# Mixer B's recurrence: E's product over the whole array, and the outputs of four steps in one PSUM bank

## The chip, the core and the metric

The kernel runs on one core of a Trainium2 chip, in one launch. The metric is the device time of that launch in microseconds (us); several runs are taken and their median is compared. TensorE (PE) multiplies matrices and writes to PSUM, eight banks of 512 float32 values on each of 128 partitions. VectorE (DVE) and ScalarE (ACT) read and write PSUM and the on-chip memory SBUF, GpSimd (POOL) only SBUF; SyncE (SP) issues most of the transfers. Each engine works through its own queue in order, and semaphores tie the queues together.

## What is computed

One inference step of a two-layer backbone over 128 prompt tokens and 1024 latent tokens, model width 1024, all in float32. Layer 0 has windowed attention (mixer A) beside a bidirectional recurrence (mixer B), layer 1 differential attention (mixer C); each layer has a modulated norm ahead, a gate, an out projection and a residual. This case is about mixer B: 8 heads of 64 channels, forward and backward. The reference for one direction:

```python
def rwkv_scan(S0, r, decay, kk, a, k, v, reverse):
    def step(S, inp):
        r_t, w_t, kk_t, a_t, k_t, v_t = inp
        sa = jnp.einsum('bhvk,bhk->bhv', S, -kk_t)
        S = (S * w_t[:, :, None, :] + sa[..., None] * (kk_t * a_t)[:, :, None, :]
             + v_t[..., None] * k_t[:, :, None, :])
        return S, jnp.einsum('bhvk,bhk->bhv', S, r_t)
```

The outputs of both directions are added, normed, gated and go into layer 0's out projection.

## The kernel before

**Chunks and items.** The recurrence isn't run token by token but in chunks of 64. Within a chunk the dependence between tokens is a triangular system; its inverse R is formed ahead for all chunks, so that a *step* of the scan handles a chunk by a few matrix products. An `Item` is 512 tokens in either direction: items 0 to 7 are the two halves of the latent sequence for each of four pairs of heads (8 steps each, both directions in one step), item 8 is the prompt of all four pairs (four lanes of two chunks, 8 steps in all). The two heads of a pair lie on the two halves of the 128 partitions. So there are 72 steps; 68 of them have a state coming in, the first step of each prompt lane has none.

**Stages of an item.** `b_prep` makes decays, keys and queries. `b_front` (once a direction) transposes them on PE into `py` tiles (L988), forms the products between keys and queries of a chunk in a `pa` tile of two banks (L998), and masks them on DVE (L1004 to `za`, L1006 to `q`), two tiles of 128 tokens at a time. `b_subst` transposes `za` to `mp` on DVE (L1032) and solves 32 by 32 blocks on POOL, 62 small instructions in a row (L1039, L1041). `b_invert` turns these back on DVE (L1050), completes R by two rounds of small products (L1061, L1068), forms E from R in another `pa` tile (L1081, scaled by DVE at L1085), and R's product with the values, which becomes `VU` (L1095). `b_scan` is the recurrence. `b_finish` norms and gates two items' sum.

**A step of the scan** (`b_scan`, L1101 to L1145), for both directions d:

- E's product, L1115: E of the chunk (64 columns) against the state G, to half the partitions of a `sc` bank; DVE adds it to `VU` (L1116).
- The update of the state, L1119: `kb` against `VU`, 128 by 128; DVE adds the old state (L1126), ACT scales it by the decay to the next S (L1128). The next step's E's product needs G.
- The outputs, to a `py` tile: S against the queries `zr` (L1132, 128 columns), then `VU` against `q` for either head (L1134, 64 columns, one half of the partitions each). For each direction DVE adds the 64 columns to `y` (L1140) or, where nothing is there yet, ACT copies them (L1142).

**PSUM before:** `pa` 2 tiles of 2 banks, `py` 2 of one bank (transposes, low-rank products, modulation and the scan's outputs share them), `sc` 2 of one bank. All eight banks are taken. Beside item 7 `out_part` multiplies the first half of layer 0's out projection, in `pa` tiles of two halves (L770 to L783).

**What sets the order.** While item i is scanned, item i+1 is inverted, item i+2 goes through front and substitution and item i+3 through prep; a hand-written table of times (`TIMES`, `T7`, `T8`, in shares of an item) interleaves the generators' steps in `timeline`. From that program a scheduler with a model of the engines' times makes each engine's queue, so neighbours on a queue can stand in another order than in the code; two products into one bank keep their order. The scan's products thus lie between pieces of fronts, inversions and the modulation (L287, `adaw`), which fills PE throughout. `mp`, `rp` and `Rt` have one buffer each; L1050 is also put behind the last DVE instruction of the neighbouring items' earlier work by a manual order (`behind`).

Of the kernel before, what the change touches and what calls it, by code (L numbers as in the profile page):

```python
# [13 lines left out]
AF = mybir.ActivationFunctionType  # L14
# [5 lines left out]
P = 128  # L20
# [121 lines left out]
def hybrid_step(ctx: ExitStack, tc: tile.TileContext, I, O, stop=99):  # L142
    nc = tc.nc
    PE, VE, AE, GE, SP = nc.tensor, nc.vector, nc.scalar, nc.gpsimd, nc.sync
    def behind(ins, others):
        """issue ins after the others, earlier instructions of its engine"""
        for o in others:
            if o is not None:
                tc.add_manual_dep(ins.ins, o.ins.name, mybir.DependencyInfo(
                    mybir.DependencyClass.NoSync, mybir.DependencyReason.DATA), reason="order")  # L150
# [36 lines left out]
    def zipped(a, na, b, nb):  # L187
        """both generators to their ends, in step"""
# [74 lines left out]
    # ------------------------------------------------------------ modulation  # L263
# [48 lines left out]
    def mod_gate(l, psum, tag, rows):  # L312
        """the gates' rows to DRAM"""
# [6 lines left out]
    # ------------------------------------------------------------ pre-norm, transposed and split  # L320
# [3 lines left out]
    def normed(xs, pool):  # L324
        """three tiles of rows over their root mean squares, in place"""
# [8 lines left out]
    def modulated(i, xs, pool, psum, hh, hl):  # L334
        """the three tiles transposed, modulated and split, to third i of the tokens"""
# [12 lines left out]
    # ------------------------------------------------------------ projections, three passes  # L348
# [60 lines left out]
    # ------------------------------------------------------------ layer 0, part 1: projections and mixer A  # L409
# [22 lines left out]
    def low_rank(m, z, pool):  # L432
        """half z of the inputs of the low-rank products to lowT, split and one part above the other"""
# [11 lines left out]
    def lora_split(z, pool):  # L445
        """both parts of the weights of half z of the low-rank products to loraT, each twice"""
# [94 lines left out]
    def a_group(g, hh, hl, wp, rp, ap, psum, rope, idb, msk):  # L541
        """mixer A of four heads, in steps: a tile is projected, its queries and keys are turned a step later, its
        scores follow when the next tile's keys are there, and its values behind them"""
# [37 lines left out]
        def near(t):  # L581
            """runs of keys, values, and masks (column, kind) of the queries of tile t"""
# [140 lines left out]
    # ------------------------------------------------------------ out projections  # L723
    RA, RB = VE, VE

    class Out:
        """weights and gates of the out projection of layer l, in pools to be closed"""
# [6 lines left out]
        def load_first(s, pool):  # L734
            """the first four steps of the contraction, to tiles that mixer C's weights take over"""
# [7 lines left out]
        def load(s, n):  # L743
            """the next n steps of the contraction"""
# [12 lines left out]
    def out_lhs(t, yT, ks, pool):  # L757
        """rows ks of tile t of the transposed input, split"""
# [8 lines left out]
    def out_part(out, pool, psum):  # L767
        """the product over the first half of the rows, to out.part"""
        for t in PART:
            yh, yl = out_lhs(t, yT0, range(4), pool)  # L770
            yield
            ps = tl(psum, [P, 2, 512], "pa")
            for j in range(2):
                w = slice(512 * j, 512 * j + 512)
                for k in range(4):
                    wh, wl = out.w[k]
                    PE.matmul(ps[:, j], yh[:, k], wh[:, w], start=k == 0, stop=False)
                    PE.matmul(ps[:, j], yh[:, k], wl[:, w], start=False, stop=False)
                    PE.matmul(ps[:, j], yl[:, k], wh[:, w], start=False, stop=k == 3)
# [6 lines left out]
    def out_tile(out, t, yT, res, pool, banks):  # L786
        """rows of token tile t behind a layer, in steps"""
# [40 lines left out]
    def out_rows(out, pool, psum):  # L828
        """the rows behind layer 0, to x1d and out.done"""
# [7 lines left out]
    # ------------------------------------------------------------ layer 0, part 2: mixer B  # L837
# [12 lines left out]
    class Item:  # L850
        """512 tokens of mixer B in either direction: half the latent sequence of one pair of heads (chunks of 64 in
        line), or the prompt of all four pairs (lanes of two chunks)."""
# [6 lines left out]
        def lanes(s, d):  # L859
            """(pair, columns, tokens)"""  # L860
# [4 lines left out]
        def chunks(s, x, d, scan=False):  # L865
            """[P, 512] in the order of the tokens (or of the scan) as [P, tiles, 2, 64] in the order of the scan"""
# [16 lines left out]
    def lanes_of(it, x, dram, blk, tok):  # L883
        """the item's columns x and its rows in DRAM, of blocks from blk on"""
# [3 lines left out]
    def b_prep(it, d, pool, pre, ps_y, rmask):  # L888
        """decays, and keys and queries under them, in direction d"""
# [72 lines left out]
    def b_front(it, d, pool, pre, ps_y, ps_a, vmask):  # L962
        """the products between the keys and queries of a chunk, and what the recurrence needs in its layout"""
# [80 lines left out]
    def b_invert(it, Rt, pool, pre, ps_s, ps_a):  # L1044
        """the rest of R with two products; then R against what enters before the state"""
# [29 lines left out]
        VE.tensor_scalar(De[:, :, 1:8:w], it.D[:, :, 0:7:w], -0.5, None, op0=ALU.mult)  # L1075
        it.E = tl(pool, [P, 2, 8, 64], "E", bufs=2)
# [7 lines left out]
        for e in range(2):  # L1084
            VE.tensor_tensor(it.E[:, :, 1 - e:8:2].rearrange("p d x t -> p (d x) t"),  # L1085
# [15 lines left out]
    def b_scan(it, lanes, H0, ring, ps_s, ps_y):  # L1101
# [5 lines left out]
        for i in range(it.steps):  # L1107
            for l in lanes:
                x, a = (l, i) if it.nl > 1 else (i // 2, i % 2)
                c, e = 2 * x + a, half_of(1 - a)  # L1110
                ps = tl(ps_s, [P, 2, 2, P], "sc")
                pu, ph = ps[:, 0], ps[:, 1]
                if G[l] is not None:
# [656 lines left out]
```

## Time and profile before

| | |
|---|---|
| runs | 2337.44, 2331.44, 2338.34 us; median 2337.44 us |
| span of the profiled execution, first to last instruction | 2335.5 us (its time with what lies around the span isn't shown apart; the median is 1.9 us above the span) |
| mean granted TensorE clock | 0.930 |
| PE busy / weight loads | 2138.4 / 1852.4 us |
| DVE / ACT / POOL busy | 1558.2 / 1052.9 / 645.2 us |
| steps of the scan | first L1115 at 689.7 us, last L1134 at 1267.8 us |

The page counts an engine as busy while one of its instructions runs. A matmul in float32 makes two weight loads (PEld) and two matmul records, so 4 records of L1119 are the products of both directions. In a form like `128*64 128x64` the first pair are the rows and columns of the array that are used, the second the partitions and elements of the result. The view of windows gives each engine's busy time in a stretch with the mean clock granted; the timeline merges neighbouring instructions of one line, and shows in brackets how long the engine sat idle before them and what ended that.

### The profile page before, as it was taken

The numbers are of one execution on the slowest core, as the hardware profiler recorded it, in microseconds if no ns is written. First come the engines' busy times: TensorE is split into PE (matmuls) and PEld (weight loads), VectorE is DVE, ScalarE is ACT, GpSimd is POOL, SyncE is SP. The second block draws the span as 40 slices with busy tenths as digits, with TensorE's granted clock in tenths as the row PEclk, the third lists the DMA queues.
The fourth block names the chain that finished last, engine by engine and source line by source line (L and its number), as shares of the span: only waits on it lengthen the run. The fifth ranks groups of instructions, "written<-read, shape, count | busy, mean of one in ns | idle before, by whom it ended". The sixth has DMA issues, their size and how long they took to land. (4 is left out here: it accounts for less than half of the span.)

```text
span 2335.5 us, 41112 instructions
## 1 busy us (share of the span) xinstructions
PE 2138.4 (92%) x15258; PEld 1852.4 (79%) x15258; DVE 1558.2 (67%) x3892; ACT 1052.9 (45%) x2862; POOL 645.2 (28%) x897
## 2 busy tenths in 40 slices
PE   7899998997769999989899789999999999998798
PEld 4899988996456666767677678899989999897676
DVE  3455545446555777875755976778887878887743
ACT  3433334333333444443424445556555565555621
POOL 0232222220332444553320432322122122211212
PEclk9999999999777889995799899999999999999899
DMA  7421213114242353433246633001010000101233
GB/s 265 140 73 58 86 47 106 65 49 155 68 131 70 111 158 101 134 115 95 69 136 191 203 122 97 26 28 45 12 49 26 28 28 26 43 12 59 78 101 118
DMA packets 164649, 205.73 MB, mean 88 GB/s; under 512 B 16193, under 2 KB 107745, under 8 KB 164449
## 3 DMA queue, kind: packets, MB, share of 16 engines
q1 hardware_dynamic: 161584, 198.25, 26.8%
q10 hardware_dynamic: 2864, 4.85, 0.6%
q8 instruction: 121, 1.98, 0.4%
q14 instruction: 80, 0.65, 0.1%
HBM read 152.32 MB, written 50.74 MB: 87 GB/s over the span
## 5 line engine op out<-in xcount | busy, mean ns | idle before, releaser
L1475 ACT ACTIVATE p<-s,mx 128x384 f32<-128x384 f32 (+1 forms) x400 | 225.1, 572 | 124.9 <-DVE mx L1472 101.2
L1470 DVE TENSOR_REDUCE mc<-s 128x1 f32<-128x384 f32 x384 | 205.6, 552 | 37.1 <-PE s L1468 33.8
L1468 PE MATMUL s<-kst,qs 128*128 128x384 f32 x768 | 202.0, 364 | 18.0 <-ACT p L1475 17.2
L352 PE MATMUL ps<-wch,hh 128*128 128x384 f32 x576 | 205.8, 358 | 10.3 <-DVE hh L1620 8.0
L1039 POOL TENSOR_TENSOR tmp<-mp,rp 128x126 f32<-128x126 f32 (+22 forms) x279 | 124.8, 447 | 301.3 <-DVE mp L1032 241.4
L353 PE MATMUL ps<-wcl,hh 128*128 128x384 f32 x576 | 198.6, 345 | 5.1 <-POOL wcl L261 5.1
L354 PE MATMUL ps<-wch,hl 128*128 128x384 f32 x576 | 196.8, 342 | 0.2
L366 PE MATMUL ps<-hh,wgh 128*128 128x384 f32 x504 | 174.7, 347 | 6.4 <-DVE bo L234 6.4
L367 PE MATMUL ps<-hl,wgh 128*128 128x384 f32 x504 | 173.7, 345 | 0.0
L368 PE MATMUL ps<-hh,wgl 128*128 128x384 f32 x504 | 173.0, 343 | 0.0
L399 POOL TENSOR_TENSOR q<-ropea,ropeb 128x256 f32<-128x256 f32 x56 | 43.1, 769 | 450.0 <-DVE ropeb L396 306.7
L1468 PEld LDWEIGHTS s<-kst,qs 128*128 128x128 f32 x768 | 130.5, 195 | 36.6 <-ACT p L1475 28.8
L261 POOL TENSOR_TENSOR wgl<-raw,wgh 128x1024 fp32r<-128x1024 f32 (+1 forms) x37 | 72.9, 1971 | 278.9 <-ACT wgh L260 263.5
L1041 POOL TENSOR_TENSOR rp<-rp,tmp 128x126 f32<-128x126 f32 (+22 forms) x279 | 134.9, 483 | 21.9
L352 PEld LDWEIGHTS ps<-wch,hh 128*128 128x128 f32 x576 | 110.5, 192 | 16.7 <-issue 11.9
L1352 DVE TENSOR_TENSOR al<-pt,ah 128x512 fp32r<-128x512 f32 (+2 forms) x168 | 100.7, 616 | 34.2 <-ACT ah L1351 32.8
L1351 ACT CAST ah<-pt 128x512 fp32r<-128x512 f32 (+2 forms) x168 | 86.4, 534 | 80.4 <-PE pt L1506 78.5
L353 PEld LDWEIGHTS ps<-wcl,hh 128*128 128x128 f32 x576 | 110.2, 191 | 7.5 <-POOL wcl L261 6.8
L261 POOL TENSOR_TENSOR wcl<-raw,wch 128x512 fp32r<-128x512 f32 x48 | 63.9, 1339 | 171.8 <-DVE csv L1171 89.7
L354 PEld LDWEIGHTS ps<-wch,hl 128*128 128x128 f32 x576 | 109.8, 191 | 1.5 <-DVE hl L1621 1.0
L1506 PE MATMUL pt<-cst,p 128*128 128x128 f32 x584 | 97.1, 281 | 6.7 <-DVE p L1488 4.3
L366 PEld LDWEIGHTS ps<-hh,wgh 128*128 128x128 f32 x504 | 96.6, 192 | 8.3 <-DVE bo L234 7.0
(411 smaller groups left out, 5958.1 us busy)
## 6 DMA issues: line engine op xcount, KB each, us to landing
hb<-pbT SPq DMA_DIRECT2D x90, 256.0 KB, 4.5
adaw<-in_ada_w_dram SPq DMA_DIRECT2D x64, 256.0 KB, 3.3
raw<-in_wc_dram SPq DMA_DIRECT2D x48, 256.0 KB, 2.7
adaw<-in_ada_w_dram SPq DMA_DIRECT2D x8, 1024.0 KB, 11.9
pbT<-bm SPq DMA_DIRECT2D x16, 512.0 KB, 2.7
low<-lowT SPq DMA_DIRECT2D x16, 512.0 KB, 4.8
raw<-in_wo_dram SPq DMA_DIRECT2D x32, 256.0 KB, 2.7
raw<-in_wpb_dram SPq DMA_DIRECT2D x13, 512.0 KB, 3.6
```

Of the source, the lines that this page charges most:

```text
L261: eng.tensor_tensor(lo[:, j:j + w], raw[:, :w], hi[:, j:j + w].bitcast(F32), ALU.subtract)
L352: PE.matmul(ps[:, :n], hh[:, k, s], wh[:, k], start=k == 0, stop=False)
L353: PE.matmul(ps[:, :n], hh[:, k, s], wl[:, k], start=False, stop=False)
L354: PE.matmul(ps[:, :n], hl[:, k, s], wh[:, k], start=False, stop=k == KT - 1)
L366: PE.matmul(ps[:, :THIRD], wh[:, k], hh[:, k, s], start=k == 0, stop=False)
L367: PE.matmul(ps[:, :THIRD], wh[:, k], hl[:, k, s], start=False, stop=False)
L368: PE.matmul(ps[:, :THIRD], wl[:, k], hh[:, k, s], start=False, stop=k == KT - 1)
L1039: eng.tensor_tensor(tv, mp[:, j:j + 1, 0:j].to_broadcast([P, n, j]), rpb[:, t:16, j:j + 1].to_broadcast([P, n, j]), ALU.mult)
L1041: eng.tensor_tensor(rpb[:, t:16, 0:j], rpb[:, t:16, 0:j], tv, ALU.add)
L1468: PE.matmul(s[c][:, :w], qs[:, e, z], hd.kp[:, z] if own else hd.kst[:, z, w * c:w * c + w], start=e == 0, stop=e == 1)
L1470: VE.tensor_reduce(mc[:, c:c + 1] if nb > 1 else mx, s[c][:, :w], axis=AX.X, op=ALU.min)
L1475: AE.activation(e[:, w * c:w * c + w], s[c][:, :w], AF.Exp, scale=-1.0, bias=mx, accum_out=sums[:, z, c:c + 1])
```

## The change

Three things, all in mixer B, and the PSUM that they need. Docstrings and comments are taken out as well, with the line numbers kept as far as L1075.

1. **E's product.** E of a chunk is stored at the other parity, so that the E of the two chunks of a tile stand side by side and the pair is one 128 by 128 operand. The product yields both halves of the partitions; as before only the half of this chunk is added to `VU`.
2. **Outputs.** A tile `yb` [128, 2 directions, 4 chunks, 64], one bank, takes four steps (for the prompt: two lanes of two chunks). In every step S against `zr` is written for both directions one behind the other; the first product of a group starts the bank, the others go on in it. Behind the fourth step a new function `outputs` issues the 16 half-width products of the four steps, and adds or copies 256 columns a direction to `y`.
3. **PSUM.** `py` gets 3 tiles instead of 2 and moves into the pools that close early, `pa` 1 instead of 2, the new `yb` 1, `sc` stays at 2. `out_part` uses one-bank `py` tiles, one for each half of its columns.

```diff
@@ out_part
-            ps = tl(psum, [P, 2, 512], "pa")
             for j in range(2):
+                ps = tl(psum, [P, 512], "py")
...
-                (AE.copy if j else VE.tensor_copy)(o, ps[:, j])
+                (AE.copy if j else VE.tensor_copy)(o, ps)
@@ b_invert
-            VE.tensor_tensor(it.E[:, :, 1 - e:8:2].rearrange("p d x t -> p (d x) t"),
+            VE.tensor_tensor(it.E[:, :, e:8:2].rearrange("p d x t -> p (d x) t"),
@@ b_scan
+        order = [(i, l) for i in range(it.steps) for l in lanes]
+
+        def outputs(yp, waiting, o):
+            rev = lambda v, d: v[..., ::-1] if d else v
+            for k, (x, a, slots) in enumerate(waiting):
                 for d in range(2):
+                    for h in range(2):
+                        PE.matmul(yp[half_of(h), d, slots[d]], it.VU[:, x, d, a, half_of(h)],
+                                  rev(it.q[d][:, 2 * x + a, h], d), start=False, stop=d == 1 and len(waiting) == k + 1)
+            for d in range(2):
+                yv = it.y[:, o[d]:o[d] + 256]
+                ypd = yp[:, d].rearrange("p n t -> p (n t)")
+                if o[d] in it.done:
+                    VE.tensor_tensor(yv, yv, ypd, ALU.add)
+                else:
+                    AE.copy(yv, ypd)
+                    it.done.add(o[d])
+
+        for n, (i, l) in enumerate(order):
...
+            if n % 4 == 0:
+                yp, waiting, begun = tl(ps_b, [P, 2, 4, 64], "yb"), [], False
...
-                    for d in range(2):
-                        PE.matmul(pu[e, d], it.E[:, d, c], G[l][:, d], start=True, stop=True)
-                    VE.tensor_tensor(it.VU[e, x, :, a], it.VU[e, x, :, a], pu[e], ALU.add)
-                yp = tl(ps_y, [P, 2, 64], "py")
+                for d in range(2):
+                    PE.matmul(pu[:, d], it.E[:, d, 2 * x:2 * x + 2].rearrange("p a t -> p (a t)"), G[l][:, d],
+                              start=True, stop=True)
+                VE.tensor_tensor(it.VU[e, x, :, a], it.VU[e, x, :, a], pu[e], ALU.add)
...
+            if S[l] is not None:
                 for d in range(2):
-                    if S[l] is not None:
-                        PE.matmul(yp[:, d], S[l][:, d], rev(it.zr[d][:, x, 1, 1 - a]), start=True, stop=False)
-                    for h in range(2):
-                        PE.matmul(yp[half_of(h), d], it.VU[:, x, d, a, half_of(h)], rev(it.q[d][:, c, h]),
-                                  start=S[l] is None, stop=True)
-                for d in range(2):
-                    o = part_of(it, d).start + P * it.tile_at(x, d) + 64 * (1 - a if d else a)
-                    yv = it.y[:, o:o + 64]
...
+                    z = it.zr[d][:, x, 1, 1 - a]
+                    PE.matmul(yp[:, d, slots[d]], S[l][:, d], z[..., ::-1] if d else z, start=not begun, stop=False)
+                    begun = True
+            waiting.append((x, a, slots))
+            if n % 4 == 3:
+                outputs(yp, waiting, o)
@@ the pools of mixer B
-        ps_a = early.enter_context(space("bpa", 2, space=PSUM, side="right"))
-        ps_y = ph2.enter_context(space("bpy", 2, space=PSUM))
+        ps_y = early.enter_context(space("bpy", 3, space=PSUM, side="right"))
+        ps_a = early.enter_context(space("bpa", 1, space=PSUM, side="right"))
         ps_s = ph2.enter_context(space("bps", 2, space=PSUM))
+        ps_b = ph2.enter_context(space("bpb", 1, space=PSUM))
```

More of the change, by code (lines that the diff above doesn't have):

```diff
@@ new lines, in b_scan @@
+        for n, (i, l) in enumerate(order):
+            x, a = (l, i) if it.nl > 1 else (i // 2, i % 2)
+            c, e = 2 * x + a, half_of(1 - a)
+            if n % 4 == 0:
+                yp, waiting, begun = tl(ps_b, [P, 2, 4, 64], "yb"), [], False
+                o = [part_of(it, d).start + (P * l if it.nl > 1 else 64 * (4 - i if d else i)) for d in range(2)]
+            slots = [2 * (l - lanes[0]) + (1 - a if d else a) if it.nl > 1 else (3 - n % 4 if d else n % 4)
+                     for d in range(2)]
+            ps = tl(ps_s, [P, 2, 2, P], "sc")
+            pu, ph = ps[:, 0], ps[:, 1]
+            if G[l] is not None:
+                for d in range(2):
+                    PE.matmul(pu[:, d], it.E[:, d, 2 * x:2 * x + 2].rearrange("p a t -> p (a t)"), G[l][:, d],
+                              start=True, stop=True)
+                VE.tensor_tensor(it.VU[e, x, :, a], it.VU[e, x, :, a], pu[e], ALU.add)
+            for d in range(2):
+                PE.matmul(ph[:, d], it.kb[d][:, c], it.VU[:, x, d, a], start=True, stop=True)
+            Gn, Sn = ring("G"), ring("S")
+            for h in range(2):
+                s = half_of(h)
+                if S[l] is None:
+                    VE.tensor_copy(Gn[s, :, s], ph[s, :, s])
+                else:
+                    it.tail = VE.tensor_tensor(Gn[s, :, s], S[l][s, :, s], ph[s, :, s], ALU.add)
+            for d in range(2):
+                AE.activation(Sn[:, d], Gn[:, d], AF.Copy, scale=it.D[:, d, c:c + 1])
+            if S[l] is not None:
+                for d in range(2):
+                    z = it.zr[d][:, x, 1, 1 - a]
[4 more added lines that the diff above has]
+                outputs(yp, waiting, o)
+            S[l], G[l] = Sn, Gn
+            yield
@@ L1242, in scan_all @@
             if it.nl == 1:
-                yield from b_scan(it, [0], H0, ring, ps_s, ps_y)
+                yield from b_scan(it, [0], H0, ring, ps_s, ps_b)
                 return
             for lanes in ([0, 1], [2, 3]):
-                yield from b_scan(it, lanes, None, ring, ps_s, ps_y)
+                yield from b_scan(it, lanes, None, ring, ps_s, ps_b)
                 for l in lanes:
@@ L1312, in hybrid_step @@
                 w0.op = w0.stage.enter_context(space("opo", 2, side="right"))
-                parts = out_part(w0, w0.lhs, ps_a)
+                parts = out_part(w0, w0.lhs, ps_y)
             t = TIMES[min(i + 2, 2) if i < 5 else 3]
```

32 lines of the change are left out of this document (4 added, 28 removed).

## The prediction

> **What bounds the kernel now.** I read the page first, then the windows of mixer B, one from each item's first L1119 to the next, then the waits, then the timeline. From the page:
>
> ```profile
> span 2335.5 us, 41112 instructions
> ...
> PEclk9999999999777889995799899999999999999899
> ```
>
> Sums are made against the span; the median of the runs shown, 2337.4 us, is 1.9 us above it, so a difference in the span is taken off the median. The low digits of the clock lie at slices 11 to 22, which is mixer B. Its windows, items 0 to 7 (stretch, busy time of each engine, clock):
>
> ```profile
> core 0: us, PE busy (x) PEld busy (x) DVE busy (x) ACT busy (x) POOL busy (x), PEclk, DMA share, GB/s
> ...
> 690.00:766.00 76.00, 69.16 (x677) 51.23 (x675) 48.26 (x82) 31.25 (x93) 32.56 (x62) 0.78 0.36 108
> 766.00:832.00 66.00, 63.82 (x670) 45.85 (x671) 47.27 (x98) 26.95 (x71) 33.57 (x72) 0.85 0.41 122
> 832.00:894.00 62.00, 58.41 (x669) 43.11 (x667) 51.44 (x104) 29.83 (x89) 25.49 (x55) 0.91 0.42 126
> 894.00:962.00 68.00, 62.85 (x673) 46.87 (x673) 46.85 (x96) 26.52 (x72) 31.95 (x69) 0.87 0.39 117
> 962.00:1021.00 59.00, 55.21 (x668) 41.15 (x667) 52.72 (x105) 30.34 (x89) 27.87 (x57) 0.97 0.46 141
> 1021.00:1091.00 70.00, 65.39 (x631) 50.36 (x631) 39.01 (x82) 23.12 (x65) 26.52 (x63) 0.73 0.23 68
> 1091.00:1160.00 69.00, 58.93 (x624) 45.80 (x624) 53.59 (x111) 32.94 (x103) 28.21 (x57) 0.78 0.31 95
> 1160.00:1246.00 86.00, 83.36 (x643) 62.77 (x644) 44.74 (x107) 28.09 (x56) 23.43 (x53) 0.96 0.48 153
> ```
>
> PE is busy for 85% to 97% of every window, and an item takes 59 us at a clock of 0.97 and 70 us at 0.73: PE bounds, and its clock sets the pace. But PE isn't alone. DVE and the substitution on POOL form a loop from item to item:
>
> ```profile
> DVE Rt L1050 <- POOL rp L1041: 17.6, 4, 8.3
> ```
> ```profile
> 875.74 1.95 DVE L1032 STREAM_TRANSPOSE mp<-za 32x1024 f32<-32x1024 f32 x1
> ...
> 919.28 4.25 DVE L1050 STREAM_TRANSPOSE Rt<-rp 32x512 f32<-32x512 f32 x4 [2.89 <-POOL rp L1041]
> ...
> 938.37 1.92 DVE L1032 STREAM_TRANSPOSE mp<-za 32x1024 f32<-32x1024 f32 x1
> ```
> ```profile
> 924.31 0.24 PE L1061 MATMUL sc<-hb,za 32*32 32x32 f32 x2 [3.29 <-DVE hb L1056]
> ...
> 927.83 1.23 PE L1119 MATMUL sc<-VU,kb 128*128 128x128 f32 x4
> ...
> 942.82 0.71 PE L1119 MATMUL sc<-VU,kb 128*128 128x128 f32 x4
> ```
> ```profile
> 925.00:942.00 17.00, 17.00 (x201) 13.12 (x204) 7.93 (x19) 5.86 (x16) 0.00 (x0) 0.50 0.39 120
> ```
>
> Four times DVE stands at L1050 until POOL has ended the substitution (17.6 us in all; one is before the scan). From the first transpose for POOL to L1050 lie 43.5 us (919.28 - 875.74), which can't shrink where L1050 waits; from there to the next item's first transpose 19.1 us. Behind that wait PE stood 3.29 us, and for the next 17 us its clock was 0.50: the same four records took 1.23 us, not 0.71.
>
> **The change part by part.** *PE time of a step.* Weight loads in order of time (start, duration, line; a group's cost is the distance to the next start):
>
> ```profile
> 804.78 0.41 PEld L1115 LDWEIGHTS sc<-G,E 128*64 128x64 f32 x4 [0.22 <-ACT S L1128]
> 805.36 0.30 PEld L1132 LDWEIGHTS py<-zr,S 128*128 128x128 f32 x2 [0.17 <-ACT mrow L289]
> 805.72 0.26 PEld L1068 LDWEIGHTS sc<-Rt,hb 32*32 32x32 f32 x10
> 806.02 0.54 PEld L1013 LDWEIGHTS py<-VU,za 64*64 64x64 f32 x16
> 806.64 0.52 PEld L1119 LDWEIGHTS sc<-VU,kb 128*128 128x128 f32 x4
> 807.28 0.20 PEld L1134 LDWEIGHTS py<-q,VU 128*64 128x64 f32 x4
> 807.54 0.30 PEld L1132 LDWEIGHTS py<-zr,S 128*128 128x128 f32 x2
> 807.91 0.20 PEld L1134 LDWEIGHTS py<-q,VU 128*64 128x64 f32 x4
> 808.17 0.92 PEld L1068 LDWEIGHTS sc<-Rt,hb 32*32 32x32 f32 x53
> ```
> ```profile
> 898.65 0.52 PEld L1119 LDWEIGHTS sc<-VU,kb 128*128 128x128 f32 x4
> 899.09 0.30 PEld L1132 LDWEIGHTS py<-zr,S 128*128 128x128 f32 x2
> 899.47 0.20 PEld L1134 LDWEIGHTS py<-q,VU 128*64 128x64 f32 x4
> ```
>
> A step now costs .58 (L1115) + .36 + .64 (L1119) + .26 + .37 + .26 = 2.47 us at full clock. L1119 costs .64 ahead of a form of another width, but .44 ahead of L1132 of its own form: changing the array's form costs .20. Afterwards E, both products of S and the update all have the form 128*128. E ahead of the pair of S: .44 + .22 (half of .44) + .38 = 1.04; the update .64; 32 half-width records each fourth step: by the nearest row, L1013, 16 records cost .62, of which I take .15 as the change of form and .47 as the flow, so 2 x .47 + .15 = 1.09, or .27 a step. Sum 1.95, saved .52. Both ends: if E and S never stand together, .20 less (.32); if the update too finds a neighbour of its form, .20 more (.72). I take .52, since the pair S is ready while E's result waits for DVE, which is where one L1132 stands now. Over 56 steps in items 0 to 6: 29 us at full clock; divided by the mean clock of their windows (.84): 35 us, 5 us an item.
>
> Against the wider E: the Trainium skill, "TensorE: Matmul & The Clock Gate", section "LDWEIGHTS (loading the stationary operand)", says that loading takes time by the number of columns. By that E's four loads would go from 53 to 107 ns each, an estimate of .21 us a step, 14 us over 68 steps, and 15 us would be left of the gain. The rows speak for .06 (.64 against .58): the product streams 128 columns in both forms and hides the load. The measurement decides.
>
> *How much of it reaches the end.* By the 43.5 and 19.1 us above, 30% of the 5 us (1.5) falls behind L1050 and counts; 70% (3.5) falls where POOL runs. Three of seven items wait for POOL already and lose that part; of the other four I take half. 3 x 1.5 + 4 x 3.2 = 17 us. Item 7, 8 steps, PE busy 83.4 of 86 us beside `out_part`: 8 x .52 = 4 us. Item 8 is the tail and a chain of latencies: nothing, with outputs some 0.5 us later.
>
> *Outputs on DVE and ACT.*
>
> ```profile
> L1004 DVE TENSOR_TENSOR za<-pa,cstones 128x256 f32<-128x256 f32 x72 | 27.8, 417 | 19.4 <-PE pa L998 16.9 <-DMA yT<-gt 2.0
> L989 ACT COPY kb<-py 128x256 f32<-128x256 f32 x72 | 27.1, 376 | 46.8 <-PE py L988 46.5
> L1140 DVE TENSOR_TENSOR y<-y,py 128x64 f32<-128x64 f32 x72 | 12.7, 217 | 14.0 <-PE py L1134 13.1 <-ACT S L1128 0.5
> L1142 ACT COPY y<-py 128x64 f32<-128x64 f32 x72 | 12.0, 215 | 77.3 <-PE py L1134 77.0 <-issue 0.3
> ```
>
> 72 adds of 217 ns become 18 of 417: 15.6 - 7.5 = 8 us of DVE less; ACT 15.5 - 6.8 = 9 us less. DVE is busy 52.7 of 59 us in the best window, so a part counts: 3 us (ends 0 and 8).
>
> *One bank for outputs.* The first S product of the next four steps waits until both halves of `yb` are read. Behind it on PE stand the update and all the filler; the scan waits for them. A step lasts some 7 us (59/8), the reading under 1, so it is hidden, unless DVE itself stands at L1050. I take 2 us for 18 groups; ends 0 and 3 stalls of 3 us.
>
> *One `pa` instead of two.* L998 of the second pair of tiles now waits for the first pair's masks; behind it stand transposes, and L1004, then L1032 and POOL wait for it.
>
> ```profile
> 918.06 0.71 PE L998 MATMUL pa<-zr,kbt 64*128 64x128 f32 x8
> ...
> 930.82 0.68 DVE L1006 TENSOR_TENSOR q<-pa,cstones 128x512 f32<-128x512 f32 x1
> ...
> 937.77 0.68 DVE L1006 TENSOR_TENSOR q<-pa,cstones 128x512 f32<-128x512 f32 x1
> ```
>
> Here the second pair's products ran ahead at 918, while the first pair was read only at 931.5. With one tile, 16 records (2 x .71, 2.4 at half clock) go between 931.5 and 937.8, where 6.3 us are free. If PE takes them at once little is lost; if they stand behind a stall like the 3.29 us, up to 4.3 us an item. I take 0.5 for 9 items: 5 us. The third `py`, which the scan leaves, costs nothing and may pay for it. `out_part` has three banks in place of four, but frees each by itself: nothing. No transfer is added or moved.
>
> **Sum:** 17 + 4 + 3 - 2 - 5 = 17 us off: 2337.4 - 17 = **2320 us**.
>
> **The rivals.** *PE alone bounds.* If the planner moves the transposes for POOL forward with the rest, all of 35 + 4 + 3 counts: 2295 us. For it: four of seven items don't wait at L1050. Against it: 43.5 us of POOL's loop stay.
>
> *The clock eats it.* PE with less work stands still more often at L1050. One such stand brought 17 us at 0.50, which costs 17 x (1 - .71/1.23) = 7 us; in three more items 21 us: 2341 us, no change. For it: the stand and the low clock are neighbours in the rows. Against: the shares of E and S fill the array better. The Trainium skill, same page, "Part 1: The HAM clock gate (the "warmup" mystery)", has this rule: an idle window of some 3.4 us halves the clock. The trace agrees with 3.29 us and 0.50.
>
> *One `pa` delays POOL*, the slower side. If the second pair's products are late by 4.3 us in each of 9 items, POOL's loop grows by 39 us where now 5 are booked; the other terms are worth 22: 2337.4 - 22 + 39 = 2354 us. It decides from 22/9 = 2.4 us an item on. For it: before, both tiles were in use at the same time from 918 to 931. Against: 6.3 us of room.
>
> *The form change isn't saved*, as the planner sets other work between: .32 instead of .52 a step, 60% of 21 us, 2328 us; counted within the forecast.
>
> **How the numbers follow.** About 0.3%, 7 us, is what a measurement of this kernel tells from no change. Forecast (2305 to 2330): .45; PE alone: .20; clock: .15; one `pa`: .20. So faster .65, same .15, slower .20. The range leaves out half of either outer rival: 2290 to 2352.
>
> **What would show it.** Right: the groups of E, S and update follow each other without .20 gaps; S against `zr` in two neighbours; half-width records 32 at a time; windows of items 0 to 6 shorter by 2 to 3 us in the mean; L1050's wait for POOL above 17.6 us. Wrong: if that wait falls while the time falls, PE alone was the bound; if the distance from L1006 to the first L1032 and from masks to products grows, it is `pa`; if PEclk in the windows drops below .84 with the same waits, the clock took the gain.

## The result, and the profile after

| | before | after |
|---|---|---|
| median of 4 runs | 2335.4 us | 2375.5 us |
| ratio, with its 95% interval | | 1.0165 [1.0132, 1.0198] |
| profiled execution, span | 2335.5 us | 2362.9 us |

The changed kernel is slower by 1.65%, some 39 us; 17 us less had been forecast. The profiled execution after is the fastest of its four, so the two spans show only 27.4 us of the loss. From the page of after:

```profile
span 2362.9 us, 40947 instructions
...
PE 2109.9 (89%) x15258; PEld 1864.3 (79%) x15258; DVE 1556.2 (66%) x3838; ACT 1044.5 (44%) x2808; POOL 644.1 (27%) x897
...
PEclk9999999998877887795889899999999999999799
```

PE is busy for less time, as intended: 2138.4 - 2109.9 = 28.5 us less, and that at a mean clock of 0.919, where it was 0.930. Yet the time rose, so less work on PE doesn't by itself make this kernel faster. The windows of items 0 to 6, each from its first L1143 (L1119 before) to the next, with the same columns as before:

```profile
693.00:764.00 71.00, 58.43 (x674) 47.09 (x675) 48.88 (x85) 29.74 (x80) 31.48 (x62) 0.81 0.43 130
764.00:837.00 73.00, 60.14 (x674) 48.68 (x672) 45.28 (x85) 27.18 (x74) 32.45 (x71) 0.80 0.34 100
837.00:905.00 68.00, 61.27 (x667) 49.04 (x667) 51.51 (x102) 27.99 (x74) 28.56 (x57) 0.80 0.40 120
905.00:981.00 76.00, 65.00 (x672) 52.48 (x670) 45.51 (x85) 26.94 (x74) 31.95 (x69) 0.72 0.34 104
981.00:1043.00 62.00, 53.20 (x669) 41.98 (x669) 51.38 (x102) 28.20 (x75) 28.66 (x58) 0.94 0.47 141
1043.00:1117.00 74.00, 60.60 (x641) 50.00 (x641) 43.70 (x77) 27.40 (x78) 29.33 (x63) 0.71 0.25 72
1117.00:1183.00 66.00, 53.52 (x611) 44.19 (x611) 48.21 (x103) 28.42 (x79) 22.43 (x49) 0.81 0.24 74
```

PE is now busy for 81% to 90% of a window, where it was 85% to 97%; it stands more. The seven windows add up to 490 us, where they were 470. DVE's wait at L1050, from the view of waits (us in all, times, the longest), and one turn of the loop through POOL, the same as was shown before, from DVE's timeline:

```profile
DVE Rt L1050 <- POOL rp L1041: 41.6, 5, 18.5
```
```profile
885.97 3.84 DVE L1032 STREAM_TRANSPOSE mp<-za 32x1024 f32<-32x1024 f32 x2
...
929.93 4.21 DVE L1050 STREAM_TRANSPOSE Rt<-rp 32x512 f32<-32x512 f32 x4 [5.97 <-POOL rp L1041]
...
938.58 0.76 DVE L1004 TENSOR_TENSOR za<-pa,cstones 128x256 f32<-128x256 f32 x2 [1.74 <-PE pa L998]
...
940.40 0.69 DVE L1006 TENSOR_TENSOR q<-pa,cstones 128x512 f32<-128x512 f32 x1
...
955.22 0.75 DVE L1004 TENSOR_TENSOR za<-pa,cstones 128x256 f32<-128x256 f32 x2
955.89 0.68 DVE L1006 TENSOR_TENSOR q<-pa,cstones 128x512 f32<-128x512 f32 x1
...
956.86 3.84 DVE L1032 STREAM_TRANSPOSE mp<-za 32x1024 f32<-32x1024 f32 x2
```

Before, this turn took 43.5 us from L1032 to L1050 and 19.1 us from there to the next L1032. Now it takes 44.0 (929.93 - 885.97) and 26.9 (956.86 - 929.93). POOL's part can't shrink; DVE only stood longer at its end. The other part grew by 7.8 us, and what stands right ahead of L1032 is the masking of the second pair of tiles, 955.22. Why so late? PE's timeline of the same stretch:

```profile
925.46 1.91 PE L287 MATMUL py<-adaw,sc 128*2 128x128 f32 x16
934.92 0.31 PE L1061 MATMUL sc<-hb,za 32*32 32x32 f32 x2 [7.55 <-DVE hb L1056]
...
949.44 1.23 PE L998 MATMUL pa<-zr,kbt 64*128 64x128 f32 x8
...
954.37 0.80 PE L998 MATMUL pa<-zr,kbt 64*128 64x128 f32 x4
```
```profile
935.00:964.00 29.00, 28.87 (x307) 23.46 (x311) 12.24 (x24) 7.35 (x20) 0.00 (x0) 0.50 0.22 67
```

With a single `pa` tile the products of the second pair (949.44) can start only when the first pair's masks have read it (940.40 + 0.69), and in PE's queue they came 8 us later still, behind other work. Before, they had run at 918 to 920, ahead of L1050 (the row at 918.06, and this one), and only masks were left:

```profile
919.45 0.72 PE L998 MATMUL pa<-zr,kbt 64*128 64x128 f32 x8
```

Now masks, products and masks stand one behind another on the way to POOL, in a stretch that PE goes through at a clock of 0.50 after it had stood for 7.55 us behind DVE's wait. POOL does nothing in those 29 us.

One number follows the loop through all of mixer B: the start of the first and of the last L1032, in the view of one line's instructions. Before, then after:

```profile
L1032 DVE STREAM_TRANSPOSE mp<-za x36: 1884/1926/1966, 610.5 to 1154.0; 32x1024 f32<-32x1024 f32 x36
```
```profile
L1032 DVE STREAM_TRANSPOSE mp<-za x36: 1882/1938/1982, 609.9 to 1179.6; 32x1024 f32<-32x1024 f32 x36
```

543.5 us became 569.7 us: 26.2 of the span's 27.4 us. I call it the *loop length* below. It has eight turns from one item's first L1032 to the next one's, and in each DVE's timeline gives two parts, parted by the first L1050. The part up to L1050, which holds POOL's work, sums to 376 us before and 356 after. The part from L1050 to the next L1032 sums to 158 us before and 206 after. So the second part grew by 48 us, in seven of the eight turns, and the first gave back 20 of them. I call the second sum the *late part*.

### The profile page after: what moved, and what is told of

Read it like the earlier page. It is cut to its first block, busy times and chain, and to the rows that moved or that the text cites. A ratio compares the mean times of both kernels' runs of the same rounds, so it can differ in the third digit from the quotient of the medians.

```text
span 2362.9 us, 40947 instructions
## 1 busy us (share of the span) xinstructions
PE 2109.9 (89%) x15258; PEld 1864.3 (79%) x15258; DVE 1556.2 (66%) x3838; ACT 1044.5 (44%) x2808; POOL 644.1 (27%) x897
## 3 DMA queue, kind: packets, MB, share of 16 engines
q1 hardware_dynamic: 161584, 198.25, 26.5%
```

## The experiments

The theory with which I went on: the one `pa` loses all that is lost, and the saving on PE is real but hidden behind the loop through POOL. Rivals: the new products or the gathered outputs lose something themselves; the clock does. Ratios below are to the kernel before on the same chip. Loop length and late part come from the one profiled execution of each kernel, which need not lie at the median: that of two_pa_sc1 is the slowest of ten (2356.8 us), that of before_poolhalf the fastest of four (2295.6 us).

| kernel | median us | ratio [95%] | loop length us | late part us |
|---|---|---|---|---|
| before | 2335.4 | 1 | 543.5 | 157.6 |
| after | 2375.5 | 1.0165 [1.0132, 1.0198] | 569.7 | 205.6 |
| pa1_only | 2371.4 | 1.0171 [1.0135, 1.0208] | 572.8 | 213.7 |
| step_pairs | 2343.1 | 1.0043 [1.0026, 1.0060] | 550.0 | 189.0 |
| two_pa_sc1 | 2343.5 | 1.0029 [1.0008, 1.0051] | 550.8 | 159.8 |
| before_poolhalf | 2306.9 | 0.9886 [0.9850, 0.9922] | 506.1 | 144.5 |
| pairs_poolhalf | 2290.1 | 0.9787 [0.9740, 0.9833] | 499.5 | 161.6 |
| after_poolhalf | 2315.1 | 0.9921 [0.9890, 0.9952] | 523.7 | 193.0 |
| before_late | 2335.9 | 1.0016 [0.9992, 1.0040] | 537.4 | 129.3 |
| pairs_late | 2333.8 | 0.9990 [0.9966, 1.0015] | 548.1 | 170.3 |
| after_late | 2343.3 | 1.0031 [1.0011, 1.0050] | 545.1 | 168.9 |
| pairs_warm | 2346.5 | 1.0038 [1.0018, 1.0058] | 549.3 | 194.3 |
| before_front | 2307.3 | 0.9896 [0.9863, 0.9929] | 511.6 | 123.0 |
| pairs_front | 2314.6 | 0.9914 [0.9882, 0.9947] | 519.8 | 141.0 |
| after_front | 2324.5 | 0.9975 [0.9944, 1.0007] | 530.0 | 149.8 |

### One `pa` tile alone

The kernel before, with one `pa` tile for fronts and inversions; the two banks that this frees serve `out_part` alone, which uses them by turns with `pa`.

```diff
-        ps_a = early.enter_context(space("bpa", 2, space=PSUM, side="right"))
+        ps_a = early.enter_context(space("bpa", 1, space=PSUM, side="right"))
+        ps_p = early.enter_context(space("bpp", 1, space=PSUM, side="right"))
@@ out_part
-            ps = tl(psum, [P, 2, 512], "pa")
+            ps = tl(psum[t % 2], [P, 2, 512], "pa")
...
-                parts = out_part(w0, w0.lhs, ps_a)
+                parts = out_part(w0, w0.lhs, (ps_a, ps_p))
```

> The kernel before with one pa tile for the fronts and the inversion instead of two; the out projection's first half keeps two tiles, everything else stays. Theory 1 (one pa tile lengthens the way from L1050 to the next item's first transpose, and with it the loop through POOL): slower by 25 to 60 us, since nothing pays for it; the distance from L1050 to the next L1032 grows from a mean of 20 us to 25 or more and DVE waits for POOL at L1050 in nearly all items. Rival (the new bank of outputs, or PE's clock after less work, costs the time): within 10 us of before.

Measured: 1.0171, 37 us more, as much as the whole change loses. Its loop:

```profile
L1032 DVE STREAM_TRANSPOSE mp<-za x36: 1887/1940/1983, 617.5 to 1190.3; 32x1024 f32<-32x1024 f32 x36
```

572.8 us, 29 more than before, with not one product of the scan changed. The way from L1050 to the next L1032 grew as expected, from a mean of 19.7 us a turn to 26.7. The other half of the expectation was missed: L1050 waits for POOL in five items and not in nearly all, and almost all of the rise from 17.6 to 27.7 us lies ahead of the scan (8.3 to 17.2):

```profile
DVE Rt L1050 <- POOL rp L1041: 27.7, 5, 17.2
```

So the loop grew by its late part, also in turns in which DVE hardly stands for POOL. The taken tile is enough to explain the loss. All the rest of the change, PE's saving and the outputs' together, then comes to nothing: 1.0165 against 1.0171.

### The new products in the old banks

The other way round: two `pa` tiles, and E over the full array, with both S products side by side, ahead of the four half-width ones; E is stored as in the change, and the outputs aren't gathered.

```diff
+                for d in range(2):
+                    PE.matmul(pu[:, d], it.E[:, d, 2 * x:2 * x + 2].rearrange("p a t -> p (a t)"), G[l][:, d],
+                              start=True, stop=True)
...
+                if S[l] is not None:
+                    for d in range(2):
+                        PE.matmul(yp[:, d], S[l][:, d], rev(it.zr[d][:, x, 1, 1 - a], d), start=d == 0, stop=False)
+                for d in range(2):
+                    for h in range(2):
+                        PE.matmul(yp[half_of(h), d], it.VU[:, x, d, a, half_of(h)], rev(it.q[d][:, c, h], d),
+                                  start=S[l] is None and d == 0, stop=d == 1)
```

> The kernel before, all its PSUM tiles kept, with E's product over the full array and, within each step, S against zr for both directions side by side ahead of all four half-width products. Theory 1: PE saves 2.47 - (1.04 + .64 + .38) = .41 us a step at full clock, some 30 us in all, and nothing is given back to pa: 8 to 25 us faster than before. Rival (PE's saving only turns into waits at L1050 and half clock): within 7 us of before or slower.

A miss: 1.0043, 9 to 10 us slower. Again PE's busy time fell, from 2138.4 to 2114.2 us at nearly the same mean clock (0.930, now 0.926), and again the time didn't:

```profile
PE 2114.2 (90%) x15258; PEld 1856.2 (79%) x15258; DVE 1555.8 (66%) x3892; ACT 1053.1 (45%) x2862; POOL 646.0 (28%) x897
```

DVE comes to L1050 sooner and waits there longer, 29.2 us instead of 17.6. The wait, and PE's timeline around another turn of the loop in this kernel:

```profile
DVE Rt L1050 <- POOL rp L1041: 29.2, 5, 8.2
```

```profile
787.15 0.71 PE L998 MATMUL pa<-zr,kbt 64*128 64x128 f32 x8
788.12 0.60 PE L287 MATMUL py<-adaw,sc 128*2 128x128 f32 x4 [0.26 <-ACT zn L991]
796.10 0.31 PE L1061 MATMUL sc<-hb,za 32*32 32x32 f32 x2 [7.38 <-DVE hb L1056]
...
815.81 0.49 PE L998 MATMUL pa<-zr,kbt 64*128 64x128 f32 x4
```

Here no bank holds the second pair back, eight of its products run at 787.15; but the last four stand in PE's queue behind the wait and much else, at 815.81, and the masks with L1032 wait for them. Around the shorter steps the queues have another order, and the late part is 31 us longer than before. So the turns shown have two ways to the same loss: a bank that isn't free, or an order in which the last of the front's products falls behind L1050.

### POOL's substitution halved

Every second round of the substitution on POOL is left out, in three kernels: before, step_pairs and after.

```diff
-        for j in range(31, 0, -1):
+        for j in range(31, 0, -2):
```

> The kernel before with every second round of the substitution on POOL left out, so POOL has half its work in an item (17 us instead of 34). Theory 1 (POOL's loop binds in about half the items of before): 15 to 40 us faster, no wait at L1050 for POOL. Rival (PE alone binds before): within 10 us.

> step_pairs with every second round of the substitution on POOL left out. step_pairs alone came out 9 us slower than before although its products take less of PE. Theory A (PE's saving is real but turns into waits at L1050, since POOL's loop sets the time; each wait ends in a stretch at half clock): without POOL's loop the saving shows, 10 to 30 us faster than the kernel before with the same rounds left out (2307 us), that is 2277 to 2297 us. Theory B (the new products or their order cost something of their own): 2307 us or more.

> The changed kernel with every second round of the substitution on POOL left out. Theory 1 (POOL's loop binds in every item of the changed kernel, and the longer way to the transposes shows only because of that): at least 40 us faster than the changed kernel, that is 0 to 30 us faster than before, and nearer to or below the kernel before with the same rounds left out. Rival (the changed kernel loses its time on PE, by stalls at the one bank or by its clock): at most 15 us faster than the changed kernel.

With the loop through POOL shortened, the kernel before gains 1.1% and step_pairs goes 17 us below it (0.9787 against 0.9886, intervals apart). PE's work, from the two pages, before_poolhalf and then pairs_poolhalf:

```profile
PE 2112.6 (92%) x15258; PEld 1832.2 (80%) x15258; DVE 1549.8 (68%) x3892; ACT 1051.1 (46%) x2862; POOL 527.7 (23%) x627
```
```profile
PE 2086.1 (91%) x15258; PEld 1835.1 (80%) x15258; DVE 1548.6 (68%) x3892; ACT 1052.5 (46%) x2862; POOL 526.2 (23%) x627
```

Here 26.5 us less of PE's busy time go with 17 us by the medians (the two profiled executions lie only 4 us apart, as that of before_poolhalf is its fastest), and with nothing where POOL's part is whole. The saving is real, and what hides it is the loop. The pages need care, though: before_poolhalf has the products of the kernel before, and PE is busy for 25.8 us less in it, at a mean clock of 0.946 instead of 0.930. Busy time counts the clock along with the work, and can be compared only where the clocks are alike, as in the two pages shown (0.946 and 0.942). The changed kernel falls by 60 us, but stays 25 us behind pairs_poolhalf (intervals apart): its one `pa`, with the gathered outputs, costs beside a faster POOL too.

### A later inversion

L1050 holds DVE for POOL while the masks of the next front stand behind it. In the table of times the start of the inversion, and so L1050, is put later by 0.08 of an item, in three kernels (one row of four shown).

```diff
-            ((-0.01, 0.85), (0.34, 1.15), (-0.08, 0.48), (0.08, 0.32), (0.06, 0.38), (0.36, 0.72), (0.75, 0.76), (0.83, 1.1), 8, (-0.1, 1.05)),
+            ((-0.01, 0.85), (0.42, 1.15), (-0.08, 0.48), (0.08, 0.32), (0.06, 0.38), (0.36, 0.72), (0.75, 0.76), (0.83, 1.1), 8, (-0.1, 1.05)),
```

> The changed kernel with the inversion's start put off by 0.08 of an item. Theory A: 10 us or more faster than the changed kernel (2375 us), though not below before, since the second pa pair of the backward front still waits for the first. Theory C: within 8 us of the changed kernel.

> step_pairs with the inversion's start in the table of times put off by 0.08 of an item, so that L1050 stands some instructions later in DVE's queue, when POOL is nearer to its end. Theory A: the waits at L1050 shrink and with them the half clock; 10 us or more faster than step_pairs (2343 us). Theory C (the place of L1050 doesn't matter, as the loop is only POOL's time and what stands between L1050 and the next transposes): within 8 us of step_pairs.

> The kernel before, with the inversion's start in the table of times later by 0.08 of an item, as in the two late kernels; nothing else. Theory A (the start before fits the order of the kernel before, which has the masks of the front ahead of L1050 already; the later start helps the changed kernels only since their masks come late): no gain, 2330 to 2350 us, L1050's waits for POOL go (7 us or so of them in items 4 and 6) but E and VU come later. Theory B (the table could be bettered for any kernel, and the gain of 32 us and 9 us says nothing of the change): 2310 to 2328 us.

The changed kernel gains 32 us, step_pairs 9 (between its two ranges), the kernel before nothing. So the later start gives back most of what the change had lost, and no more than that. The late part of the changed kernel falls from 206 to 169 us, though in every turn within the scan the masks of the last two pairs still stand behind L1050, as they did. In before_late L1050 waits for POOL only once, 3.7 us ahead of the scan, and its late part is 28 us shorter; but the part up to L1050 is 22 us longer (398 us for 376), and the time is the same. Taking away waits by putting L1050 later is in itself worth nothing. And against the kernel before with the same later start, the change as a whole now costs 0.15% (1.0031 against 1.0016, intervals that overlap), where it had cost 1.65%: what it costs hangs on the table of times.

### More work on PE

step_pairs with four products of 128 by 512, overwritten at once, ahead of L1061 in each item, meant to keep PE busy through DVE's wait.

```diff
+        for _ in range(4):
+            PE.matmul(pv.rearrange("p u t -> p (u t)"), ident, rmask, start=True, stop=True)
```

> step_pairs with four more products of 128x512 on PE ahead of L1061 in each inversion, whose results are overwritten: they keep PE at work while DVE waits at L1050. They cost 9 x 3.4 = 31 us of PE time at full clock. Theory A in its form by the clock (the idle time of PE at that wait halves the clock for 17 to 34 us): the half clock behind the waits goes, the time falls by 5 us or more or stays in spite of the added work. Rival (the clock isn't governed by that wait): slower by 10 to 30 us.

1.0038 against step_pairs' 1.0043: no difference. The mean clock rose from 0.926 to 0.939, and PE's busy time stayed (2114.9 us against 2114.2), so the added products were paid by the faster clock. They filled the wait only in part: in three turns they ran ahead of it and PE still stood for 3.65 to 5.70 us (5.90 to 7.38 in step_pairs), and the half clock still followed, in the first of these for some 10 us instead of some 20. This tells little of the bound: a time set by PE would have stayed as well. It shows only that the low clock can be bought off at no gain.

### Two `pa` tiles for the whole change

`pa` 2 and `py` 2 tiles as before, `yb` 1, paid by `sc`, which falls to 1; `out_part` as before.

```diff
-        ps_y = early.enter_context(space("bpy", 3, space=PSUM, side="right"))
-        ps_a = early.enter_context(space("bpa", 1, space=PSUM, side="right"))
-        ps_s = ph2.enter_context(space("bps", 2, space=PSUM))
+        ps_y = early.enter_context(space("bpy", 2, space=PSUM, side="right"))
+        ps_a = early.enter_context(space("bpa", 2, space=PSUM, side="right"))
+        ps_s = ph2.enter_context(space("bps", 1, space=PSUM))
```

> The change with two pa tiles again (four banks), two py, one sc and one yb; out_part in pa as before. Theory 1 (the one pa is the whole loss of the change): masks and L1032 come as in the kernel before, 2325 to 2345 us, if one sc bank costs no more than 10 us. Theory 2 (the order that the planner makes around shorter PE work loses, whatever the banks, as step_pairs lost 8 us with both pa tiles): 2343 us or more, with the fourth masks of a front again just ahead of the next L1032. A third: one sc bank puts each inversion's products behind the scan's, 2360 us or more, and says nothing of pa.

1.0029, 32 us under the changed kernel and about where step_pairs is. That fits the one `pa` as the loss, but the time doesn't part the first two theories: it lies in the range of both, and what the single `sc` costs wasn't measured by itself. The late part does part them: 160 us, as before (158), and neither 206 as in the changed kernel nor 189 as in step_pairs. With two tiles masks and L1032 come as they did before, for all that PE's steps are shorter; the loop is still 7 us longer, in the part up to L1050 (383 us for 376).

### Another table of times

Later inversion as above, and in items from the second row on the second front ends, and the substitution starts, 0.06 of an item earlier (the second front's start 0.01 earlier).

```diff
-            ((-0.01, 0.85), (0.34, 1.15), (-0.08, 0.48), (0.08, 0.32), (0.06, 0.38), (0.36, 0.72), (0.75, 0.76), (0.83, 1.1), 8, (-0.1, 1.05)),
+            ((-0.01, 0.85), (0.42, 1.15), (-0.08, 0.48), (0.08, 0.32), (0.06, 0.38), (0.35, 0.66), (0.69, 0.7), (0.83, 1.1), 8, (-0.1, 1.05)),
```

> step_pairs with the later inversion, and the second front's end and the substitution's start earlier by 0.06 of an item. Theory A (in step_pairs the fourth masks of the front, right ahead of L1032, end the way to POOL): masks and L1032 come earlier, from L1050 to the next L1032 under 18 us, 2315 to 2328 us, under the kernel before. Rival (the planner puts L998 where PE has room, and PE is full in that stretch, so the earlier start only moves other work back): 2330 to 2345 us.

> The kernel before with the table of times of pairs_front, nothing else. Theory A (the 20 us of pairs_front come from the change's products, which shorten PE, once the masks are in time): 2326 to 2345 us, so the table alone brings at most 8 us. Theory B (the table alone brings them): 2308 to 2325 us, and the products' form brings nothing.

> The changed kernel with the same table. Theory A (what the one pa costs is the lateness of the masks, and the table gives that back as it does in step_pairs): 2310 to 2335 us, at or under the kernel before. Rival (with one pa the second pair's products can't start before the first pair's masks, whatever the table asks, so that L1032 stays late): 2336 to 2350 us, about that of after_late (2343).

With it step_pairs came to 2315 us, 20 us under the kernel before, which looked like PE's saving at last. The control says otherwise: the kernel before with the same table runs in 2307 us, 25 us under its own time (ratios 0.9914 and 0.9896, alike within their intervals). Theory B of the control held, at the lower end of its range: the table's gain isn't the change's. The first and last L1032 of before_front and of pairs_front:

```profile
L1032 DVE STREAM_TRANSPOSE mp<-za x36: 1880/1924/1961, 607.4 to 1119.0; 32x1024 f32<-32x1024 f32 x36
```
```profile
L1032 DVE STREAM_TRANSPOSE mp<-za x36: 1882/1928/1955, 609.3 to 1129.1; 32x1024 f32<-32x1024 f32 x36
```

The loop is 32 us shorter than before in the one, 24 in the other. And this is what becomes of PE's saving, in the windows of items 0 to 6 (last row: sums of the length and of the busy times) and the waits at L1050, before_front and then pairs_front:

```profile
sum 452.00, PE 418.30 PEld 315.73 DVE 337.17 ACT 199.15 POOL 211.73; mean PE 59.76 PEld 45.10 DVE 48.17 ACT 28.45 POOL 30.25
```
```profile
DVE Rt L1050 <- POOL rp L1041: 2.9, 1, 2.9
```
```profile
sum 458.00, PE 402.35 PEld 321.82 DVE 338.51 ACT 198.20 POOL 213.10; mean PE 57.48 PEld 45.97 DVE 48.36 ACT 28.31 POOL 30.44
```
```profile
DVE Rt L1050 <- POOL rp L1041: 16.5, 5, 3.9
```

Sixteen us less of PE's busy time, and six us more of time: PE stands 22 us longer in these windows, and DVE's waits at L1050 grew by 13.6. The changed kernel, with the same table, stays 0.6% behind pairs_front (0.9975 against 0.9914, intervals that overlap at their ends alone) and clearly behind before_front. It is at the kernel before, not under it: the table gives back most of what the one `pa` takes, and the rest stays, as in the loop length (530.0 against 519.8). Theory A had 2310 to 2335 for it and held; that the rival's range was missed says that the masks can be brought forward in part.

## Why the prediction was wrong

**PE's work of a step: right.** Weight loads of the changed kernel in order of time, at full clock:

```profile
854.71 0.52 PEld L1139 LDWEIGHTS sc<-G,E 128*128 128x128 f32 x4 [1.55 <-issue]
855.15 0.30 PEld L1156 LDWEIGHTS yb<-zr,S 128*128 128x128 f32 x2
...
856.60 0.78 PEld L1116 LDWEIGHTS yb<-q,VU 128*64 128x64 f32 x24
857.45 0.43 PEld L1013 LDWEIGHTS py<-VU,za 64*64 64x64 f32 x12
857.95 0.52 PEld L1143 LDWEIGHTS sc<-VU,kb 128*128 128x128 f32 x4
858.59 0.31 PEld L1116 LDWEIGHTS yb<-q,VU 128*64 128x64 f32 x8
858.97 0.20 PEld L1013 LDWEIGHTS py<-VU,za 64*64 64x64 f32 x4
```

E ahead of its own form costs .44, the update ahead of another form .64, the 32 half-width records .85 + .38 = 1.23 in two pieces: .44, .64 and 1.09 had been booked. The 29 us at full clock that had been booked for items 0 to 6 can't be set against the 28.5 us of the page, since the clock fell as well. Busy time multiplied by the clock, window by window, gives 363 us before and 328 after: by this estimate some 36 us were saved, rather more than booked. Against the rule of the Trainium skill ("TensorE: Matmul & The Clock Gate", section "LDWEIGHTS (loading the stationary operand)") that loading goes by columns, the trace agrees that E's four loads are longer (.52 against .41), but the step doesn't feel it: E costs what the update of its own form costs, .44.

**How much of it reaches the end: here the prediction failed.** "PE bounds, and its clock sets the pace" was read from busy shares of 85% to 97%, and 24 us (17 + 4 + 3) were let through to the end. The runs show none: step_pairs is 9 to 10 us slower with 24 us less on PE, pairs_front no faster than before_front with 16 us less in the windows. Only with POOL's part halved did 26.5 us bring 17. The prediction did see the loop L1032, POOL, L1050, L1032, and then booked 30% of PE's saving behind L1050 as a sure gain and half of what four items saved ahead of it. But behind L1050 it isn't the amount of PE's work that counts but which products and masks stand there, and when: this late part grew where it should have shrunk, from 158 us to 189 in step_pairs and 206 in the changed kernel. The windows, forecast to be 2 to 3 us shorter in the mean, are 2.9 us longer (490 us for 470).

**One `pa`: mechanism right as a rival, price wrong in the sum.** 0.5 us an item had been booked; alone it costs 37 us, 4.1 an item, and the rival had put it at up to 4.3 with a chance of 0.20. It decides from 2.4 an item on, so the time had to come out above. "6.3 us are free" was the failing step: the free time between the two pairs' masks was taken from a profile in which the products lay ahead. With one tile, 14 us pass from the end of the first pair's masks (941.09) to the start of the second's (955.22), as the products stand behind other work, at half clock. That 4.1 comes so near to 4.3 is in part luck: the late part grew by 7.0 us a turn in pa1_only, and the part up to L1050 gave 3.1 of them back. And it is the price with this table of times: with the later inversion the whole change costs 0.15%, with the third table 0.8% (0.9975 against 0.9896), each against the kernel before with the same table; one `pa` alone was run with neither. The 32 us more for this term and the 24 us that didn't come make 56, and the forecast was 55 us too low.

**The sum of the rival:** 2354 us were given for it, 2375 came, since the 22 us that it left to the other terms didn't come either (2335 + 37 is 2372).

**Outputs on DVE and ACT: price right, saving booked too high, no gain seen.** From the groups of after:

```profile
L1122 DVE TENSOR_TENSOR y<-y,yb 128x256 f32<-128x256 f32 x18 | 6.9, 418 | 4.7 <-PE yb L1116 3.5 <-ACT y L1124 1.1
```
```profile
L1124 ACT COPY y<-yb 128x256 f32<-128x256 f32 x18 | 5.9, 374 | 20.7 <-PE yb L1116 20.6
```

The mean durations (418 and 374 ns) are as booked. But the sum took the number times the mean, where the busy column of the same rows is lower, as neighbours overlap in the trace: it went from 12.7 to 6.9 us on DVE and from 12.0 to 5.9 on ACT, so 5.8 and 6.1 us were saved and not 8 and 9. On the two pages DVE is busy for 2.0 us less in all, ACT for 8.4.

**One bank for outputs: no loss seen.** After and pa1_only are alike within their intervals, so gathering, with 2 us booked, costs no more than PE's saving hides. `py`'s other place costs nothing ahead of the scan: the first L1032 starts at 609.9 us against 610.5.

**The clock** did fall, from a mean of .84 in the windows (by their lengths) to .79, and the waits at L1050 within the scan rose from 9.3 to 23.1 us (less the one ahead of it, 8.3 and 18.5). But it isn't where the loss comes from: the rival had it follow from less work on PE, and pa1_only, with PE's work unchanged, loses as much. How much of each late part is due to the half clock stays open, since pairs_warm brought more work along with the faster clock.

What also stays open: why the order around the shorter steps makes the late part of step_pairs longer even with both tiles, beyond the one stretch shown; what one `sc` costs; and which of the table's two shifts wins before_front its 25 us (the later inversion alone brought none, so it needs the earlier front; that by itself wasn't run).

## What to carry to other kernels

A busy share of 90% doesn't make an engine the bound where a loop over several engines returns to it: find the loop, and count of a saving only what lies on its late side. A buffer that two uses overlap in is priced by what then stands in series on that loop, not by the gap seen while both were there; and the price holds for one schedule only: the same change cost 1.65% with one table of times, and 0.15% and 0.8% with two others. And before a gain is put down to a change, give the same new schedule to the kernel before: here the table alone brought 25 us, and the kernel before with that table is as fast as any that leaves nothing out.

## What was unexpected of the hardware

The half clock lasted far longer than the stand that it followed. PE stood 7.55 us, and then ran at 0.50 through 29 us in which it was busy for 28.87 of them (935 to 964 us); before, 17 us followed a stand of 3.29 us. The Trainium skill ("TensorE: Matmul & The Clock Gate", section "Part 1: The HAM clock gate (the "warmup" mystery)") has it that one busy window of some 3.4 us gives the full clock back. These rows don't agree: 29 us of a PE that the profile calls busy didn't. What the gate counts as busy can't be seen in them.
